# A decoder layer in one kernel: the down-projection's fast passes reordered, and its last two column chunks made a fourth fast pass

## The chip, the cores and the metric

The kernel runs on one core of one Trainium2 chip. It is one program that computes a whole decoder layer for 256 tokens. The metric is the device time of one execution in microseconds (us). An engine name in the profile stands for: PE TensorE's matmuls, PEld its weight loads, DVE VectorE, ACT ScalarE, POOL GpSimd, SP SyncE, which issues most of the transfers.

## The reference

The layer has a token mixer (two kinds of attention side by side) and a channel mixer. Only the end of the channel mixer is touched by the change:

```python
h = rmsnorm(x, pre_ffn_g[l])
u = causal_dwconv(h @ w_up[l], conv_w[l], conv_b[l])          # 2048 -> 2 x 5632
gate, val = jnp.split(u, 2, axis=-1)
y = (jax.nn.gelu(gate, approximate=True) * val) @ w_down[l]   # 5632 -> 2048
x = x + rmsnorm(y, post_ffn_g[l])
```

There are 256 tokens, in two tiles of 128. Everything is float32. The last line needs the mean square over all 2048 columns of y for each token, so no token's output can be written before its whole row of y is known.

## The kernel before

**Products in three matmuls.** Every float32 matrix product is made of three reduced-precision matmuls: each operand is split into a high part (a cast on ScalarE) and a low part (source minus high part, on VectorE), and high x high, high x low and low x high are added up in PSUM. `product` (L964) does this for a 128x128 block on the left and up to 512 columns on the right; `mm3` (L305) does the same in the plain passes. `split` (L311) makes a pair of parts, and so does `w_split` (L102) behind `w_unit` (L120). The split weights lie in two rings `whi` and `wlo` of five buffers each; a buffer is free when TensorE has read it for the last time.

**Two halves.** The 5632 inner columns are done in two halves of 22 tiles of 128. In each half, 11 turns of the up-projection (two weight groups each, gate and value) make the 22 tiles `G[0..21]`, by matmul, convolution, GELU and product; the convolution works in a tile called `room`. Then the half's part of the down-projection is done, in passes over column ranges of `w_down`. Partial results gather in `y_sb`.

**A fast pass.** `fast_pass` (L969) covers 1024 columns. It goes over 11 pairs of inner tiles. A plain pair needs 2x2x2 = 8 products (two inner tiles, two token tiles, two column chunks), 24 matmuls of 512 columns. For the four pairs in `FAST` it uses a Strassen-like scheme with seven products, 21 matmuls: the four sums of token tiles are made once per half by `token_sums` and kept in `sums`, and four differences of the weight blocks (L1004 to L1010, into the tile `tb`) are made on VectorE for each pair in each pass, then split like weights. Of the seven products, four gather in the PSUM banks `early`, whose sums are added to `y_sb` by `add_early` when the last fast pair is done; the others gather in the banks `late`, together with the plain pairs, and are added block by block by `add_late` in the pass's last pair.

**Which passes there are.** Half 0 has two fast passes (columns 0 to 1023, 1024 to 2047). Half 1 has one fast pass (0 to 1023), then a plain pass over chunk 2 (columns 1024 to 1535), then the plain pass over chunk 3 (1536 to 2047), which is written out separately at the end. In the first pass of each half the pairs come in the order 1, 0, 3, 2, 5, 4, 7, 6, 8, 9, 10, in the others from 0 to 10.

**The last chunk.** It does token tile 0 for all 11 pairs first, and the other tile for the first five pairs (`LAST = 11 - HOLD`, `HOLD = 6`), in two halves of 256 columns with a bank each. The split weights of the last six pairs are kept (four in the rings, two in rooms that are free by then, `rest`). While these last products of token tile 1 run on TensorE, tokens 0 to 127 are finished.

**Finishing.** In half 1, `down` (L1074) takes a finished bank: VectorE adds it to `y_sb`, ScalarE squares it and sums up the row (`ysq`), and GpSimd multiplies it by the gain `gbf` (L1079). When a token tile has all its columns, `before_last` and `rstd_y` make the inverse root (VectorE, then a power on GpSimd), and `finish` (L1162) multiplies, adds the residual `x_back` and writes out.

**Transfers.** Weights come in pieces of 512 KB on SP's queue, in order. In the fast passes eight buffers take turns: five of the ring `raw`, two of `extra`, one third of `tb` (which lies in the convolution's `room`). The residual comes back from `x_dram` into `x_back`, two transfers of 1 MB, during the last passes; it lies in the room that `sums` had.

**What sets the order.** TensorE's order is the program's own throughout. On the other engines a planner orders the instructions by its own estimate of when each can start, up to the last stage (from the second `manual_schedule`); from there all engines keep the program's order.

Of the kernel before, what the change touches and what calls it, by code (L numbers as in the profile page):

```python
# [17 lines left out]
P = 128  # L18
# [7 lines left out]
FHALF = 22  # L26
HOLD = 6
FAST = (0, 2, 4, 6)
# [3 lines left out]
def hybrid_layer(ctx: ExitStack, tc: tile.TileContext, x, pre_mix_g, w_in, b_forget, sinks,  # L32
# [16 lines left out]
    def bank(tag="acc"):  # L49
        return ps.tile([P, 512], F32, tag=tag, bufs=4, name="bank_" + tag)  # L50
# [796 lines left out]
    with tc.tile_pool(name="ffn", bufs=1) as fp:  # L847
# [115 lines left out]

        def product(b, lh, ll, rhs, cols, first, last):  # L964
            hi, lo = rhs
            for i, (a, r) in enumerate(((lh, hi), (lh, lo), (ll, hi))):
                pe.matmul(b, a, r[:, cols], start=(first and i == 0), stop=(last and i == 2))  # L967

        def fast_pass(G, sums, order, k00, c0, load, tb, early, late, add_early, add_late):  # L969

# [6 lines left out]
            def parts(src, n):  # L977
                hi, lo = w_parts(n)
# [5 lines left out]
            started = set()  # L984

            def first(bk):
                new = id(bk) not in started
                started.add(id(bk))
                return new

            for u in order:
                k = 2 * u
                ra, rb = (load(w_rows(w_down, k00 + k + a, 1, c0, UNIT)) for a in range(2))
                if u in FAST:
# [38 lines left out]

        ysq = [small.tile([P, 5], F32, tag=f"ysq{t}", bufs=1, name=f"ysq{t}") for t in range(2)]
        gbf = None
        for half in range(2):
# [44 lines left out]

            LAST = FHALF // 2 - HOLD
            extra = fp.tile([P, 2, UNIT], F32, tag="gbc", name="extra")
# [11 lines left out]

            for n in range(0, 2 if half else 4, 2):
                early, late = ([bank(tag) for _ in range(4)] for tag in ("acc", "att"))
                order = list(range(FHALF // 2))
                if n == 0:
                    order[:8] = [1, 0, 3, 2, 5, 4, 7, 6]  # L1100

                def y_of(t, c):
                    return y_sb[:, t, (n + c) * 512:(n + c + 1) * 512]
# [20 lines left out]

                def add_late(t, c, b):
# [5 lines left out]
                fast_pass(G, sums, order, half * FHALF, n * 512, load, tb, early, late, add_early,  # L1131
                          add_late)
            for n in range(2, 2 + half):
                b2 = [bank(), bank()]
                for u in range(FHALF // 2):
                    hi, lo = w_unit(w_rows(w_down, half * FHALF + u * 2, 2, n * 512, 512), 2, 512)
                    for a in range(2):
                        k = u * 2 + a
                        for t in range(2):
                            mm3(b2[t], G[k], t, hi[:, a, :], lo[:, a, :], slice(0, 512), k == 0,  # L1140
                                k == FHALF - 1)
                for t in range(2):
                    down(t, n, b2[t])

# [17 lines left out]
        def finish(t, cs, r, q, y=None):  # L1162
# [3 lines left out]

        rest = [fp.tile([P, 2, UNIT], F32R, tag="gbc", name="rest"),
                fp.tile([P, ROOM], F32R, tag="room", name="rest")[:, 544:544 + 2 * UNIT]
                .rearrange("p (a c) -> p a c", a=2)]
        x_back = main.tile([P, 2, D], F32, tag="x", name="x_back")  # L1170
        b0, b1 = bank(), [bank(), bank()]
        halves = [slice(0, 256), slice(256, 512)]
        held = []
        for u in range(FHALF // 2):
            if u in (1, 2):
                sp.dma_start(x_back[:, u - 1, :], x_dram[(u - 1) * P:u * P, :])
            hi, lo = w_unit(w_rows(w_down, FHALF + u * 2, 2, 1536, 512), 2, 512,
                            keep=(None, [rest[u - LAST][:, i, :] for i in range(2)])
                            if LAST <= u < FHALF // 2 - 4 else None)
            for a in range(2):  # L1180
                k = u * 2 + a
                args = (k, hi[:, a, :], lo[:, a, :])
                held.append(args)
                mm3(b0, G[k], 0, *args[1:], slice(0, 512), k == 0, k == FHALF - 1)
                for h in range(2 if u < LAST else 0):
                    mm3(b1[h][:, halves[h]], G[k], 1, *args[1:], halves[h], k == 0, False)
# [49 lines left out]
```

## Time and profile before

| | us |
|---|---|
| median of 3 runs | 1079.45 |
| lowest and highest | 1078.14, 1080.15 |
| the profiled execution's own time | 1077.63 |
| its span, first to last instruction | 1075.6 |
| half 0's two fast passes | 584.05 to 644.50, 644.50 to 701.78 |
| half 1's fast pass | 944.05 to 1006.06 |
| its plain passes over chunks 2 and 3 | 1006.06 to 1067.08 |
| after TensorE's last matmul | 1067.08 to 1075.60 |

Times in the lines of the profile are microseconds from the start of the span; in a line of the timeline the first number is the start, the second the length of the stretch, and `x3` the number of instructions in it. What stands in brackets is how long the engine was idle before it and which instruction ended that. Matmuls are pipelined, so a single one is listed with 0.39 us although one starts every 0.23.

### The profile page before, as it was taken

How to read it: one execution, taken by the hardware profiler on the slowest of the kernel's cores; microseconds unless marked ns; L12 is line 12 of the kernel's file. 1: busy time of each engine (PE TensorE's matmuls, PEld its weight loads, DVE VectorE, ACT ScalarE, POOL GpSimd, SP SyncE). 2: the span in 40 equal slices, each digit the busy share in tenths (PEclk: the TensorE clock that was granted, in tenths of full speed). 3: DMA queues.
4: the chain of work that ended last, by engine and by line, in shares of the span. 5: the costliest groups of instructions: out<-in, count | busy, mean ns of one | idle time of the engine just before them, and what ended most of it. 6: DMA issues, size and time to landing. Idle time of an engine off the chain costs nothing.

```text
span 1075.6 us, 16358 instructions
## 1 busy us (share of the span) xinstructions
PE 1056.9 (98%) x5950; PEld 919.1 (85%) x5950; DVE 822.4 (76%) x1336; ACT 630.7 (59%) x1087; POOL 224.9 (21%) x256
## 2 busy tenths in 40 slices
PE   9999999999999999999999999999999999989996
PEld 7899988887889888888888788888888888878886
DVE  5988878887567887788777989668777787779763
ACT  7766766666556765656554645456565555555450
POOL 4343243332022121212121000012121212100211
PEclk9999999999999999999999999999999999999998
DMA  8646556554873876656664666666566656555752
GB/s 291 206 122 177 176 157 209 162 161 157 293 236 105 283 226 195 191 184 191 192 191 138 219 206 215 214 180 194 178 213 189 187 184 198 189 192 179 280 168 79
DMA packets 157100, 207.09 MB, mean 193 GB/s; under 512 B 6844, under 2 KB 131036, under 8 KB 155996
## 3 DMA queue, kind: packets, MB, share of 16 engines
q1 hardware_dynamic: 156016, 203.37, 60.2%
q10 hardware_dynamic: 1004, 2.68, 0.6%
q8 instruction: 47, 0.77, 0.3%
q14 instruction: 33, 0.27, 0.1%
HBM read 201.68 MB, written 4.21 MB: 191 GB/s over the span
## 4 chain that ended last, share of the span: by engine, by line
PE 89%; DVE 4%; ACT 2%; DMA 2%; POOL 2%; issue 1%; SPq 0%; POOLq 0%; DVEq 0%; ACTq 0%
PE bank_acc L309 18%; PE bank_acc L284 16%; PE bank_att L284 14%; PE bank_att L967 12%; PE bank_acc L290 8%; PE bank_att L290 7%; PE bank_acc L253 4%; PE bank_acc L967 3%; PE bank_acc L258 2%; DVE wlo L115 2%; PE bank_att L475 1%; POOL scr L442 1%; PE bank_att L510 1%; PE bank_acc L932 1%; DMA x_in<-in_x_dram 1%
## 5 line engine op out<-in xcount | busy, mean ns | idle before, releaser
L115 DVE TENSOR_TENSOR wlo<-raw,whi 128x1024 fp32r<-128x1024 f32 (+3 forms) x291 | 358.6, 1242 | 133.2 <-ACT whi L112 128.5
L112 ACT CAST whi<-raw 128x1024 fp32r<-128x1024 f32 (+3 forms) x290 | 294.4, 1031 | 149.6 <-issue 88.8
L899 POOL TENSOR_TENSOR room<-room,rowf 128x256 f32<-128x256 f32 x88 | 99.4, 1150 | 393.1 <-DVE room L898 391.5
L284 PE MATMUL bank_acc<-hT,whi 128*128 128x512 f32 x736 | 173.3, 390 | 0.0
L284 PEld LDWEIGHTS bank_acc<-hT,whi 128*128 128x128 f32 x736 | 136.4, 188 | 27.4
L284 PE MATMUL bank_att<-hT,whi 128*128 128x512 f32 x640 | 150.6, 390 | 0.0
L284 PEld LDWEIGHTS bank_att<-hT,whi 128*128 128x128 f32 x640 | 118.7, 188 | 23.9
L967 PE MATMUL bank_att<-whi,G 128*128 128x512 f32 x384 | 122.5, 389 | 0.0
L290 PEld LDWEIGHTS bank_acc<-hT,wlo 128*128 128x128 f32 x736 | 89.3, 188 | 2.0
L290 PE MATMUL bank_acc<-hT,wlo 128*128 128x256 f32 x736 | 89.8, 279 | 0.0
L253 PE MATMUL bank_acc<-hT,whi 128*128 128x512 f32 x352 | 89.2, 396 | 0.0
L901 ACT ACTIVATE room<-room,cw 128x256 f32<-128x256 f32 x88 | 53.0, 602 | 60.1 <-POOL room L899 59.9
L967 PEld LDWEIGHTS bank_att<-whi,G 128*128 128x128 f32 x384 | 72.2, 188 | 15.1
L309 PE MATMUL bank_acc<-whi,oT 128*128 128x512 f32 (+1 forms) x272 | 82.5, 380 | 0.0
L290 PEld LDWEIGHTS bank_att<-hT,wlo 128*128 128x128 f32 x640 | 77.6, 188 | 1.7
L290 PE MATMUL bank_att<-hT,wlo 128*128 128x256 f32 x640 | 77.9, 279 | 0.0
L903 DVE SCALAR_TENSOR_TENSOR room<-room,cw 128x256 f32<-128x256 f32 x88 | 61.9, 703 | 19.4 <-ACT room L901 19.4
L967 PE MATMUL bank_att<-wlo,G 128*128 128x512 f32 x192 | 74.7, 389 | 0.0
L253 PEld LDWEIGHTS bank_acc<-hT,whi 128*128 128x128 f32 x352 | 62.9, 188 | 11.3
L309 PEld LDWEIGHTS bank_acc<-whi,oT 128*128 128x128 f32 x272 | 50.2, 188 | 9.3
L313 DVE TENSOR_TENSOR wlo<-raw,whi 128x1024 fp32r<-128x1024 f32 (+1 forms) x44 | 49.5, 1149 | 9.4 <-ACT whi L312 9.3
L312 ACT CAST whi<-raw 128x1024 fp32r<-128x1024 f32 (+1 forms) x44 | 42.4, 991 | 21.3 <-PE bank_att L967 15.9
(252 smaller groups left out, 1613.8 us busy)
## 6 DMA issues: line engine op xcount, KB each, us to landing
raw<-in_w_up_dram SPq DMA_DIRECT2D x176, 512.0 KB, 4.2
raw<-in_w_down_dram SPq DMA_DIRECT2D x66, 512.0 KB, 4.6
raw<-in_w_in_dram SPq DMA_DIRECT2D x51, 512.0 KB, 4.2
raw<-in_w_out_dram SPq DMA_DIRECT2D x32, 512.0 KB, 4.5
extra<-in_w_down_dram SPq DMA_DIRECT2D x15, 512.0 KB, 4.9
raw<-in_w_in_dram SPq DMA_DIRECT2D x16, 384.0 KB, 3.3
tb<-in_w_down_dram SPq DMA_DIRECT2D x7, 512.0 KB, 3.7
cb<-c_dram SPq DMA_DIRECT2D x8, 256.0 KB, 3.7
```

The costliest lines, as they stand in the source:

```text
L112: i1 = act.copy(hi[:, cs], raw[:, cs])
L115: i2 = dve.tensor_tensor(lo[:, cs], raw[:, cs], hi[:, cs].bitcast(F32), op=ALU.subtract)
L253: pe.matmul(b, parts[u][0][:, a, m * P:(m + 1) * P], hT[:, kt, :], start=(kt == 0), stop=(kt == KT - 1))
L284: pe.matmul(b, parts[u][0][:, a, m * P:(m + 1) * P], hT[:, kt, :], start=(kt == 0), stop=(kt == KT - 1))
L290: pe.matmul(b[:, 256:512], parts[u][1][:, a, m * P:(m + 1) * P], hT[:, kt, 0:256], start=False, stop=False)
L309: pe.matmul(b, a, r[:, cols], start=(first and i == 0), stop=(last and i == 2))
L312: act.copy(hi, src)
L313: dve.tensor_tensor(lo, src, hi.bitcast(F32), op=ALU.subtract)
L899: pool.tensor_tensor(u[:, 2:258], u[:, 2:258], rowf, op=ALU.mult)
L901: act.activation(y, u[:, 2:258], AF.Identity, bias=cw[:, 3, ch:ch + 1], scale=cw[:, 2, ch:ch + 1])
L903: dve.scalar_tensor_tensor(y, u[:, 1:257], cw[:, 1, ch:ch + 1], y, op0=ALU.mult, op1=ALU.add)
L967: pe.matmul(b, a, r[:, cols], start=(first and i == 0), stop=(last and i == 2))
```

## The change

- **The order in each half's first pass** becomes 1, 3, 0, 5, 2, 7, 4, 8, 6, 9, 10: two plain pairs come before the first fast one, and two instead of three are left after the last.
- **A second fast pass in half 1** over columns 1024 to 2047 takes the place of the two plain passes. It uses the same `sums`, so these stay until its last fast pair is done.
- **Its last three pairs are held** (`HOLD = 3`): they are split like the others, but their products come after all the rest, block by block (`block`): token tile 0 chunk 2, tile 0 chunk 3, tile 1 chunk 2, tile 1 chunk 3, each 18 matmuls of 512 columns, the last one as two times 18 of 256 in a bank of its own. What had gathered in the fourth bank before is added to `y_sb` on VectorE first. Four of the six held weight rows lie in the rings, the last pair's two in `rest`, which now takes the room of `sums`.
- **`add_late` is gone**: in the other passes the last pair goes through `block` too, in the same order of matmuls as before, and the banks are added after it.
- **`x_back`** lies behind the gain in the tile that took `hT`'s place, and its two transfers are issued ahead of the fourth pass's loads.
- **The finish** has two more `down` steps, those of chunk 2, in the program's own order between the blocks.

```diff
-HOLD = 6
+HOLD = 3
...
-        def product(b, lh, ll, rhs, cols, first, last):
+        def product(b, lh, ll, rhs, cols, first, last, to=None):
             hi, lo = rhs
             for i, (a, r) in enumerate(((lh, hi), (lh, lo), (ll, hi))):
-                pe.matmul(b, a, r[:, cols], start=(first and i == 0), stop=(last and i == 2))
+                pe.matmul(b[:, to] if to else b, a, r[:, cols], start=(first and i == 0),
+                          stop=(last and i == 2))
...
-                b = [parts(ra, UNIT), parts(rb, UNIT)]
-                blocks = ((p2, 0, left), (p3, 0, right), (p4, 1, left), (p22, 1, right))
-                end = u == order[-1]
-                order2 = ([(a, x) for x in blocks for a in range(2)] if end else
-                          [(a, x) for a in range(2) for x in blocks])
-                for a, (bk, t, cols) in order2:
-                    product(bk, *of(k + a, t), b[a], cols, first(bk), end and a == 1)
-                    if end and a == 1:
-                        add_late(t, 1 if cols is right else 0, bk)
+                b = [parts(r, UNIT, keep[a] if keep and u == order[-1] else None)
+                     for a, r in enumerate((ra, rb))]
+                if u in order[-hold:]:
+                    held += [(k + a, b[a]) for a in range(2)]
+                    continue
+                for a in range(2):
+                    for bk, t, cols in blocks:
+                        product(bk, *of(k + a, t), b[a], cols, first(bk),
+                                hold > 1 and bk is p22 and u == order[-hold - 1] and a == 1)
+
+            def block(i, bk=None, cols=None):
+                b, t, c = blocks[i]
+                for n, (k, w) in enumerate(held):
+                    product(bk or b, *of(k, t), w, cols or c, bk is not None and n == 0,
+                            n == len(held) - 1, cols and slice(cols.start - 512, cols.stop - 512))
+
+            return block
...
-                gbf = main.tile([P, 4 * D], F32, tag="hT", name="gbc_ffn")[:, 0:D]
+                late_room = main.tile([P, 4 * D], F32, tag="hT", name="late_room")
+                gbf = late_room[:, 0:D]
+                x_back = late_room[:, D:3 * D].rearrange("p (t c) -> p t c", t=2)
...
-            for n in range(0, 2 if half else 4, 2):
+            for n in (0, 2):
                 early, late = ([bank(tag) for _ in range(4)] for tag in ("acc", "att"))
                 order = list(range(FHALF // 2))
                 if n == 0:
-                    order[:8] = [1, 0, 3, 2, 5, 4, 7, 6]
+                    order[:9] = [1, 3, 0, 5, 2, 7, 4, 8, 6]
+                elif half:
+                    for t in range(2):
+                        sp.dma_start(x_back[:, t, :], x_dram[t * P:(t + 1) * P, :])
...
+                final = half and n
+                rest = None
+                if final:
+                    rest = main.tile([P, 2, 2, UNIT], F32R, tag="x", name="rest")
+                block = fast_pass(G, sums, order, half * FHALF, n * 512, load, tb, early, late,
+                                  add_early, HOLD if final else 1,
+                                  rest and [[rest[:, a, i, :] for i in range(2)]
+                                            for a in range(2)])
+                if final:
+                    dve.tensor_tensor(y_of(1, 1), late[3], y_of(1, 1), op=ALU.add)
+                    break
+                for i in range(4):
+                    block(i)
+                    t, c = divmod(i, 2)
                     if half:
-                        down(t, n + c, b)
+                        down(t, n + c, late[i])
                     else:
-                        dve.tensor_tensor(y_of(t, c), b, y_of(t, c), op=ALU.add)
...
-            for n in range(2, 2 + half):
-                b2 = [bank(), bank()]
-                for u in range(FHALF // 2):
-                    hi, lo = w_unit(w_rows(w_down, half * FHALF + u * 2, 2, n * 512, 512), 2, 512)
...
+        block(0)
+        down(0, 2, late[0])
         v = before_last(0, 3)
-        down(0, 3, b0)
+        block(1)
+        down(0, 3, late[1])
         r = rstd_y(0, 3, v)
         for n in range(4):
             finish(0, slice(n * 512, (n + 1) * 512), r, sp)
+        block(2)
+        down(1, 2, late[2])
         last = fp.tile([P, 256], F32, tag="last", name="last")
         for h in range(2):
             if h:
                 v = before_last(1, 4)
-            for k, hi, lo in held[LAST * 2:]:
-                mm3(b1[h][:, halves[h]], G[k], 1, hi, lo, halves[h], False, k == FHALF - 1)
-            down(1, 3, b1[h], h, last if h else None)
+            b = bank()
+            block(3, b, slice(512 + h * 256, 768 + h * 256))
+            down(1, 3, b, h, last if h else None)
```

More of the change, by code (lines that the diff above doesn't have):

```diff
@@ L962, in token_sums, with fast_pass @@
             split(into[:, 0:512], into[:, 512:UNIT], s.rearrange("p k c -> p (k c)"))
-        def product(b, lh, ll, rhs, cols, first, last):
+        def product(b, lh, ll, rhs, cols, first, last, to=None):
             hi, lo = rhs
             for i, (a, r) in enumerate(((lh, hi), (lh, lo), (ll, hi))):
-                pe.matmul(b, a, r[:, cols], start=(first and i == 0), stop=(last and i == 2))
-        def fast_pass(G, sums, order, k00, c0, load, tb, early, late, add_early, add_late):
+                pe.matmul(b[:, to] if to else b, a, r[:, cols], start=(first and i == 0),
+                          stop=(last and i == 2))
+        def fast_pass(G, sums, order, k00, c0, load, tb, early, late, add_early, hold=1,
+                      keep=None):
             left, right = slice(0, 512), slice(512, UNIT)
@@ L975, in of, with parts @@
                 return G[k][:, t * P:(t + 1) * P], G[k][:, 256 + t * P:256 + (t + 1) * P]
-            def parts(src, n):
-                hi, lo = w_parts(n)
+            def parts(src, n, into=None):
+                hi, lo = into or w_parts(n)
                 split(hi, lo, src)
@@ L983, in fast_pass @@
             p2, p3, p4, p22 = late
-            started = set()
+            blocks = ((p2, 0, left), (p3, 0, right), (p4, 1, left), (p22, 1, right))
+            started, held = set(), []
             def first(bk):
@@ L1080, in down @@
                                    gbf[:, n * 512:(n + 1) * 512][:, cs], op=ALU.mult)
-            LAST = FHALF // 2 - HOLD
             extra = fp.tile([P, 2, UNIT], F32, tag="gbc", name="extra")
@@ L1123, in add_early @@
                     dve.tensor_tensor(y_of(1, 1), s, y_of(1, 1), op=ALU.add)
-                def add_late(t, c, b):
+                final = half and n
[12 more added lines that the diff above has]
+                    t, c = divmod(i, 2)
                     if half:
-                        down(t, n + c, b)
+                        down(t, n + c, late[i])
                     else:
-                        dve.tensor_tensor(y_of(t, c), b, y_of(t, c), op=ALU.add)
-                fast_pass(G, sums, order, half * FHALF, n * 512, load, tb, early, late, add_early,
-                          add_late)
-            for n in range(2, 2 + half):
-                b2 = [bank(), bank()]
-                for u in range(FHALF // 2):
-                    hi, lo = w_unit(w_rows(w_down, half * FHALF + u * 2, 2, n * 512, 512), 2, 512)
[L1137 to L1143, printed above, removed]
+                        dve.tensor_tensor(y_of(t, c), late[i], y_of(t, c), op=ALU.add)
         def before_last(t, n):
@@ L1165, in finish @@
             q.dma_start(of[t * P:(t + 1) * P, cs], y_sb[:, t, cs])
[L1167 to L1186, printed above, removed]
         ctx.enter_context(tc.manual_schedule(
```

## The prediction

> **What bounds the kernel now.** I read the page's busy shares first, then what TensorE waited for, then a table by stage, then the timelines around the stages that the change touches.
>
> ```profile
> PE 1056.9 (98%) x5950; PEld 919.1 (85%) x5950; DVE 822.4 (76%) x1336; ACT 630.7 (59%) x1087; POOL 224.9 (21%) x256
> ```
>
> TensorE sets the end. Time can be won only from matmuls, from its few waits, or after its last matmul. Its waits:
>
> ```profile
> PE bank_acc L967 <- ACT whi L312: 3.7, 2, 1.9
> PE bank_acc L967 <- DVE wlo L313: 1.8, 2, 0.9
> ```
>
> L967 is the fast products; two waits each means one pair in each half's first pass. By stage (length, then busy time and count of PE, PEld, DVE, ACT, POOL, then PE clock, DMA share, GB/s):
>
> ```profile
> 584.05:644.50 60.45, 57.70 (x253) 47.23 (x252) 55.74 (x71) 32.06 (x38) 1.34 (x2) 1.00 0.57 192
> 644.50:701.78 57.28, 57.28 (x254) 47.47 (x253) 43.73 (x47) 30.23 (x32) 0.20 (x4) 1.00 0.63 211
> 944.05:1006.06 62.01, 59.26 (x253) 48.36 (x252) 53.92 (x67) 34.13 (x42) 2.80 (x4) 0.97 0.63 219
> 1006.06:1036.00 29.94, 29.94 (x133) 24.77 (x132) 18.78 (x15) 15.42 (x18) 5.34 (x3) 1.00 0.66 212
> 1036.00:1067.08 31.08, 31.05 (x199) 28.11 (x197) 14.49 (x19) 7.88 (x14) 6.10 (x5) 1.00 0.27 89
> 1067.08:1075.60 8.52, 0.00 (x0) 0.00 (x0) 3.54 (x7) 0.51 (x2) 1.27 (x2) 0.66 0.35 123
> ```
>
> Rows 1 and 2 are the two passes of half 0, row 3 the first pass of half 1, rows 4 and 5 the plain passes over column chunks 2 and 3, row 6 the tail. A fast pass has 4x7x3 + 7x8x3 = 252 matmuls of 512 columns. Row 2, with PE busy throughout, prices one at 57.28 / 252 = 0.2273 us, so a plain pair (24) lasts 5.45 and a fast pair (21) 4.77. Row 5 has 66 of 512 columns and 132 of 256: (31.08 - 66 x 0.2273) / 132 = 0.122 us for a 256.
>
> **Part 1: two plain pairs in front.** Against row 2, the same work costs 3.17 us more in row 1 and 4.73 more in row 3: 7.90 in all. In half 1 this is TensorE, and the clock after it:
>
> ```profile
> 949.96 0.39 PE L967 MATMUL bank_acc<-whi,G 128*128 128x512 f32 x1
> 952.21 0.50 PE L967 MATMUL bank_acc<-whi,sums 128*128 128x512 f32 x1 [1.87 <-ACT whi L312]
> 953.60 0.71 PE L967 MATMUL bank_acc<-wlo,sums 128*128 128x512 f32 x1 [0.88 <-DVE wlo L313]
> ```
>
> ```profile
> 954.00:957.20 3.20, 3.20 (x9) 2.43 (x9) 3.20 (x4) 2.85 (x4) 0.00 (x0) 0.51 0.27 90
> ...
> 590.00:596.00 6.00, 3.25 (x14) 2.17 (x13) 5.96 (x8) 4.61 (x5) 0.00 (x0) 1.00 0.52 179
> ```
>
> The waits of half 1 are followed by a granted clock of 0.51, those of half 0 by 1.00; this is the 1.56 us between 4.73 and 3.17. [...] I count it as going, because it follows the wait at once.
>
> Why TensorE waited: one plain pair lasts until 949.5, and VectorE is not yet there:
>
> ```profile
> 944.44 0.76 DVE L898 TENSOR_TENSOR room<-bank_acc,room 128x256 f32<-128x256 f32 x2 [4.24 <-ACT room L897]
> ...
> 948.77 0.98 DVE L313 TENSOR_TENSOR G<-room,G 128x256 fp32r<-128x256 f32 x2
> 949.79 0.69 DVE L1004 TENSOR_TENSOR tb<-raw 128x512 f32<-128x512 f32 x1
> 950.40 0.69 DVE L1005 TENSOR_TENSOR tb<-raw 128x512 f32<-128x512 f32 x1
> ...
> 952.33 2.42 DVE L313 TENSOR_TENSOR wlo<-tb,whi 128x1024 fp32r<-128x1024 f32 x2
> ```
>
> The differences (0.61 apart) need the room of the convolution, which ends at 949.75; the two split sums are there at 953.5 and 954.7. With pair 3 in between, TensorE comes to pair 0 at 944.05 + 2 x 5.45 = 954.95, wants the first sum's low part after four matmuls (955.9) and the second after nine (957.0). Slack 2.3 us at both. What is added before that: pair 3's two splits, 2 x 1.21. The ring of five split buffers lets the first be made where pair 0's quarter was made before, and the second when the last projection frees a buffer, inside the 4.24 us VectorE idles. Were all of it, and the quarter's 0.6, to come behind the convolution, the chain would be up to 3.0 later, that is 0.7 over the slack. So I take -7.90, bounds -7.90 and -6.5. Half 0 shows the same picture.
>
> Loads: the order of the first eight changes, and the eighth waits for the convolution's room on SP's queue, with all later loads behind it:
>
> ```profile
> 949.83 0.33 SPq L1093 DMA_DIRECT2D tb<-in_w_down_dram  x1
> 951.11 6.26 SPq L69 DMA_DIRECT2D raw<-in_w_down_dram  x3
> ```
>
> ```profile
> raw<-in_w_down_dram SPq DMA_DIRECT2D x66, 512.0 KB, 4.6
> ```
>
> Pair 2, formerly loads 7 and 8, becomes 9 and 10: issued 2.1 apart, the last lands at 951.11 + 2.1 + 4.6 = 957.8. TensorE needs its first sum at 944.05 + 5.45 + 5.45 + 4.77 + 5.45 + 0.9 = 966.1, and from the landing to that sum it takes 0.6 + 1.0 + 1.2. Slack over 5 us, cost nothing.
>
> **Part 2: the fourth pass.** Removed: 264 matmuls' worth in rows 4 and 5, 29.94 + 31.08 = 61.02 us. Added: 234 of 512 and, in the last block, 36 of 256: 234 x 0.2273 + 36 x 0.122 = 57.58. Difference -3.44 us: twelve products' worth of 512 columns is 2.73, the rest is the smaller number of 256s.
>
> VectorE's load grows. A fast pair needs four differences and about 3.5 splits, 2.4 + 4.2 = 6.6 us, a plain pair 2.4, together 9.0 against TensorE's 10.2. It keeps up, but at the boundary of half 1's passes it gets crowded. Pair 6 used to have three plain pairs behind it and a plain pass after them; now it has two and a fast pair. Pair 6 ended at 1006.06 - 3 x 5.45 = 989.7, and the first addition of the seven products' sums was
>
> ```profile
> 987.49 0.69 DVE L1116 TENSOR_TENSOR y_sb<-s,y_sb 128x512 f32<-128x512 f32 x1
> ```
>
> 2.2 before that end. From there VectorE has, at 0.61 an addition or difference and 1.2 a split: 8 additions 4.9, pair 10's splits 2.4, the next pair's differences 2.4, its quarter 0.6, its two sums 2.4, three late additions 1.8: 14.5 us, done 12.3 after pair 6. TensorE needs the second sum 2 x 5.45 + 9 x 0.2273 = 12.95 after it. Slack 0.65. Against it stand GpSimd's multiplications (L1079) of the first pass, which fell on idle VectorE time before:
>
> ```profile
> 1004.93 0.69 DVE L1077 TENSOR_TENSOR y_sb<-bank_att,y_sb 128x512 f32<-128x512 f32 x1 [0.57 <-PE bank_att L967]
> 1006.29 0.69 DVE L1077 TENSOR_TENSOR y_sb<-bank_att,y_sb 128x512 f32<-128x512 f32 x1 [0.67 <-PE bank_att L967]
> 1006.90 7.14 DVE L115 TENSOR_TENSOR wlo<-raw,whi 128x1024 fp32r<-128x1024 f32 x4
> ```
>
> ```profile
> 1004.60 2.55 POOL L1079 TENSOR_TENSOR y_sb<-y_sb,gbc_ffn 128x512 f32<-128x512 f32 x2 [58.31 <-ACT junk L1078]
> 1007.37 4.25 POOL L1079 TENSOR_TENSOR y_sb<-y_sb,gbc_ffn 128x512 f32<-128x512 f32 x2 [0.22 <-ACT junk L1078]
> ```
>
> Four splits took 7.14 instead of 4.8: 2.3 us lost beside 4.25 of GpSimd; the addition that reads PSUM stayed at 0.69. One to two splits before the second sum, and the ones for the rest of pair 0 and for pair 1 right after, lose 0.6 each. I take +1.3 us of waiting (about three splits' loss less the slack), bounds 0 (it fits) and 4. Half 0 has half the additions there and no multiplications: nothing.
>
> At the end of the pass, pairs 8 to 10 are held, pair 10 in the room of the token sums, so its casts on ScalarE wait for pair 6's last product, with only pair 10's second cast behind them. VectorE has from 2.2 before that: 8 additions, 5 splits and one late addition, 11.5 us, done 9.3 after pair 6; TensorE needs the last low part 5.45 + 16 x 0.2273 = 9.1 after it. About nothing; bounds 0 and 1.5. The two reads of the residual, 1.05 MB each, now stand ahead of the pass's loads on SP's queue: at 211 GB/s up to 9.9 us of traffic. The loads run eight buffers, some 20 us, ahead, so I cost them at nothing; without that cover, 9.9.
>
> **Part 3: the tail.** Now chunk 2's sums fall into it too.
>
> ```profile
> 1058.45 0.69 DVE L1077 TENSOR_TENSOR y_sb<-bank_acc,y_sb 128x512 f32<-128x512 f32 x1 [8.69 <-PE bank_acc L309]
> 1059.99 0.16 DVE L1157 SCALAR_TENSOR_TENSOR rv<-ysq,rv 128x1 f32<-128x1 f32 x1 [0.85 <-ACT junk L1078]
> 1061.87 2.74 DVE L1163 SCALAR_TENSOR_TENSOR y_sb<-y_sb,ry,x_back 128x512 f32<-128x512 f32 x4 [1.72 <-POOL ry L1159]
> ```
>
> ```profile
> 1060.04 1.29 POOL L1079 TENSOR_TENSOR y_sb<-y_sb,gbc_ffn 128x512 f32<-128x512 f32 x1 [18.51 <-ACT junk L1078]
> 1061.29 0.55 POOL L1159 TENSOR_TENSOR ry<-rv,mhalf 128x1 f32<-128x1 f32 x1
> 1065.63 0.74 POOL L1079 TENSOR_TENSOR y_sb<-y_sb,gbc_ffn 128x256 f32<-128x256 f32 x1 [3.79 <-ACT junk L1078]
> 1067.59 0.73 POOL L1079 TENSOR_TENSOR last<-y_sb,gbc_ffn 128x256 f32<-128x256 f32 x1 [1.22 <-DVE y_sb L1077]
> 1068.41 0.55 POOL L1159 TENSOR_TENSOR ry<-rv,mhalf 128x1 f32<-128x1 f32 x1
> ```
>
> Let E be TensorE's end (1067.08 here). Tokens 0 to 127 were ready at E - 8.6, their four last steps ended at E - 2.5. After the change they are ready at E - 18 x 0.2273 - 36 x 0.122 = E - 8.5, so the steps end at E - 2.4. Behind them on VectorE now come chunk 2's addition (0.7) and then the first 256's. ScalarE's square of the former ends near E - 0.8, GpSimd's 1.29 runs to E + 0.5, its two 0.74s to E + 2.0, and the power behind them ends at E + 2.5 instead of 1068.96 - 1067.08 = E + 1.9. +0.65 us, bounds +0.2 and +1.2.
>
> **Sum**, against the profiled execution's 1077.63 (span 1075.6 and 2.0 around it): -7.90 - 3.44 + 1.3 + 0.65 = -9.4, so 1068.2. The median of the runs, 1079.45, stands 1.8 above that execution; I forecast it to stay so: 1070.0.
>
> **Rivals.** (a) VectorE loses GpSimd's whole time. Rows: 2.3 of 4.25 lost, not all. If the four multiplications of 1.29 each cost VectorE their length, 5.2 less the slack of 0.65 is 4.5 of waiting, 3.2 more than forecast: 1073.2. [...] (b) The opening wait only moves to the second fast pair, because loads 9 and 10 come late. It begins at 5 us of lateness; for it speak the 6.26 us for three loads, against it that VectorE has slack everywhere after 953.6. As long as the old gaps, it gives back most of 7.90: 1077. (c) Slower than before: the residual's reads sit on SP's queue until GpSimd has finished with the gain in the same tile (1007.37 + 4.25, 5.6 us after the pass), and all loads of the fourth pass behind them. Then 9.9 of traffic, 4.6 of landing and 3.4 of preparing: 23 us of idle TensorE, about 1092; from 11 us on it decides the sign. Against it: at 1004.93 VectorE writes one slice of y_sb while GpSimd works on another, so waits go by slices.
>
> **Chances.** Forecast 0.64, own range 1068.3 to 1071.8; (a) 0.21; (b) 0.09; (c) 0.06. The range 1067.0 to 1074.5 takes in the first two and the bounds of the terms. A measurement of this kernel tells 0.2%, 2.2 us, from no change: faster 0.89, within it 0.05, slower 0.06.
>
> **What would show it.** The changed profile should have no wait of TensorE on pair 0 of the first passes, stages of 57.3 us with clock 1.00 there, TensorE ending its fourth pass 57.6 us plus any wait after the third, a wait of one to two us at that pass's first fast pair on a VectorE split, and a tail near 9.2 us. A wait of over 4 us there, a wait at pair 2 of an opening, or SP's loads stopped behind the residual would make it wrong.

## The result, and the profile after

| | before | after |
|---|---|---|
| median, us | 1078.80 (6 runs) | 1071.22 (6 runs) |
| lowest and highest | 1077.16, 1080.15 | 1070.06, 1072.17 |
| the profiled execution | 1077.63, span 1075.6 | 1070.95, span 1069.2 |

The ratio is 0.9931, with a 95% interval of 0.9918 to 0.9943: the changed kernel is 7.6 us faster. The prediction was 1070.0, with a range of 1067.0 to 1074.5.

TensorE's waits in the down-projection, from the profile after (total, number, longest):

```profile
PE bank_att L967 <- DVE wlo L313: 2.4, 2, 1.8
PE bank_att L967 <- DVE rest L313: 1.1, 2, 0.8
```

The waits of the openings, on `bank_acc`, are gone. Four others have come, all on `bank_att` and all on low parts from VectorE. The table by stage shows where they are (columns as in the prediction: stretch and length, then busy time and count of PE, PEld, DVE, ACT, POOL, then PE clock, DMA share, GB/s):

```profile
583.97:641.08 57.11, 57.11 (x253) 47.30 (x252) 53.29 (x69) 31.11 (x37) 1.79 (x2) 1.00 0.61 198
641.08:698.30 57.22, 57.22 (x253) 47.23 (x252) 45.07 (x49) 30.03 (x32) 0.20 (x4) 1.00 0.63 210
...
940.74:997.86 57.12, 57.12 (x253) 47.31 (x252) 53.68 (x70) 31.71 (x39) 2.56 (x3) 1.00 0.74 254
997.86:1060.24 62.38, 58.89 (x271) 47.81 (x269) 52.69 (x64) 30.18 (x42) 9.81 (x8) 1.00 0.38 127
1060.24:1069.20 8.96, 0.00 (x0) 0.00 (x0) 3.51 (x8) 0.51 (x2) 2.39 (x4) 0.68 0.34 117
```

Rows 1 and 3 are the two openings. Both run through at a clock of 1.00, and are 3.34 and 4.89 us shorter than before. Row 4 is the new fourth pass: 62.38 us, where the two plain passes took 61.02. It has fewer matmuls than they had and still takes 1.36 us longer. TensorE in that pass, from the timeline (start, length, and in brackets the idle time before it):

```profile
1003.44 0.50 PE L967 MATMUL bank_att<-wlo,G 128*128 128x512 f32 x1 [1.79 <-DVE wlo L313]
...
1005.67 0.50 PE L967 MATMUL bank_att<-wlo,G 128*128 128x512 f32 x1 [0.57 <-DVE wlo L313]
...
1045.24 0.97 PE L967 MATMUL bank_att<-rest,G 128*128 128x512 f32 x3 [0.31 <-DVE rest L313]
...
1046.97 0.73 PE L967 MATMUL bank_att<-rest,G 128*128 128x512 f32 x2 [0.77 <-DVE rest L313]
```

Two waits stand at the start of the pass, the first for pair 0's plain weight row (the last of the four splits that this pair needs), the second for pair 1's first row. Two stand in the first of the held blocks, for pair 10's two low parts. Each costs more than its listed length: the idle time is counted from the end of the matmul before, 0.39 us after its start, where the next would have started after 0.23, and from the matmul behind the wait to the next one it is 0.34 (1003.44 to 1003.78). From the pass's first matmul to pair 2's it takes 13.14 us (997.86 to 1011.00), where 45 matmuls at 0.2273 us are 10.23: 2.9 us lost for 2.36 us of waiting. VectorE around the first two, and GpSimd beside it, in the same profile:

```profile
996.77 0.68 DVE L1090 TENSOR_TENSOR y_sb<-bank_att,y_sb 128x512 f32<-128x512 f32 x1
997.38 2.09 DVE L313 TENSOR_TENSOR wlo<-tb,whi 128x1024 fp32r<-128x1024 f32 x1
999.39 0.68 DVE L1090 TENSOR_TENSOR y_sb<-bank_att,y_sb 128x512 f32<-128x512 f32 x1
999.99 1.18 DVE L1007 TENSOR_TENSOR tb<-raw 128x512 f32<-128x512 f32 x1
1001.09 0.68 DVE L1090 TENSOR_TENSOR y_sb<-bank_att,y_sb 128x512 f32<-128x512 f32 x1
1001.69 1.70 DVE L313 TENSOR_TENSOR wlo<-tb,whi 128x1024 fp32r<-128x1024 f32 x1
1003.31 2.31 DVE L313 TENSOR_TENSOR wlo<-raw,whi 128x1024 fp32r<-128x1024 f32 x1
```

```profile
997.09 3.53 POOL L1092 TENSOR_TENSOR y_sb<-y_sb,late_room 128x512 f32<-128x512 f32 x2 [53.40 <-ACT junk L1091]
1000.96 1.34 POOL L1092 TENSOR_TENSOR y_sb<-y_sb,late_room 128x512 f32<-128x512 f32 x1 [0.34 <-ACT junk L1091]
1002.66 1.88 POOL L1092 TENSOR_TENSOR y_sb<-y_sb,late_room 128x512 f32<-128x512 f32 x1 [0.35 <-ACT junk L1091]
```

VectorE is never idle here. A split whose two inputs lie in SBUF takes 1.22 us by itself (1015.21 in `e3_no_gain`, below) and 2.09, 1.70 and 2.31 beside GpSimd's multiplications by the gain, a difference 1.18 instead of 0.68 (1016.95 there). The additions that take one input from PSUM (L1090) stay at 0.68. The splits end at 1003.39 and 1005.62, and TensorE goes on at 1003.44 and 1005.67.

### The profile page after: what moved, and what is told of

It reads as the page before. It is cut to its first block, busy times and chain, and to the rows that moved or that the text cites. A ratio compares the mean times of both kernels' runs of the same rounds, so it can differ in the third digit from the quotient of the medians.

```text
span 1069.2 us, 16290 instructions
## 1 busy us (share of the span) xinstructions
PE 1052.4 (98%) x5890; PEld 912.9 (85%) x5890; DVE 843.4 (79%) x1369; ACT 637.2 (60%) x1096; POOL 224.8 (21%) x256
## 4 chain that ended last, share of the span: by engine, by line
PE 90%; DVE 4%; DMA 2%; issue 2%; POOL 1%; ACT 1%; SPq 0%; DVEq 0%; POOLq 0%; ACTq 0%
PE bank_acc L284 16%; PE bank_att L967 14%; PE bank_att L284 14%; PE bank_acc L309 12%; PE bank_acc L290 8%; PE bank_att L290 7%; PE bank_acc L253 6%; PE bank_acc L967 4%; PE bank_acc L258 3%; PE bank_att L475 1%; DVE wlo L313 1%; PE bank_att L510 1%; DVE wlo L115 1%; PE bank_acc L932 1%; DMA x_in<-in_x_dram 1%
## 5 line engine op out<-in xcount | busy, mean ns | idle before, releaser
L115 DVE TENSOR_TENSOR wlo<-raw,whi 128x1024 fp32r<-128x1024 f32 (+3 forms) x271 | 330.1, 1228 | 117.1 <-ACT whi L112 112.4
L112 ACT CAST whi<-raw 128x1024 fp32r<-128x1024 f32 (+3 forms) x270 | 273.3, 1029 | 124.4 <-issue 88.9
L967 PE MATMUL bank_att<-whi,G 128*128 128x512 f32 x488 | 156.2, 389 | 0.0
L967 PEld LDWEIGHTS bank_att<-whi,G 128*128 128x128 f32 x488 | 91.6, 188 | 18.9
L967 PE MATMUL bank_att<-wlo,G 128*128 128x512 f32 x244 | 95.2, 390 | 2.4 <-DVE wlo L313 2.4
L313 DVE TENSOR_TENSOR wlo<-raw,whi 128x1024 fp32r<-128x1024 f32 (+1 forms) x56 | 62.4, 1138 | 13.4 <-ACT whi L312 13.4
L312 ACT CAST whi<-tb 128x1024 fp32r<-128x1024 f32 x42 | 44.0, 1050 | 45.0 <-PE bank_att L967 19.2
L312 ACT CAST whi<-raw 128x1024 fp32r<-128x1024 f32 (+1 forms) x56 | 52.4, 958 | 28.8 <-PE bank_att L967 22.2
```

The lines of the kernel that those rows point to most:

```text
L112: i1 = act.copy(hi[:, cs], raw[:, cs])
L115: i2 = dve.tensor_tensor(lo[:, cs], raw[:, cs], hi[:, cs].bitcast(F32), op=ALU.subtract)
L312: act.copy(hi, src)
L313: dve.tensor_tensor(lo, src, hi.bitcast(F32), op=ALU.subtract)
L967: pe.matmul(b[:, to] if to else b, a, r[:, cols], start=(first and i == 0), stop=(last and i == 2))
```

## The experiments

Ratios are against the kernel before on the same chip. A fourth pass is measured from the end of half 1's first pass to VectorE's addition of the last 256 columns; the tail is the rest of the span.

**The order alone** (run `e1_order_alone`): the kernel before, with one line.

```diff
-                    order[:8] = [1, 0, 3, 2, 5, 4, 7, 6]
+                    order[:9] = [1, 3, 0, 5, 2, 7, 4, 8, 6]
```

> The kernel before with the new pair order in the two first passes, and nothing else. Theory: all of the gain of the change comes from here. Both opening waits go and the clock dip with them, so each first pass starts its next stage 57.1 us after its start: 3.3 us less in half 0, 4.9 in half 1, the rest as before: -8.2 us, ratio 0.9924. Rival (the fourth pass carries a part of the gain, and the order alone makes the plain pass behind it wait): -5 us or less, ratio 0.995 or more.

Measured: 1068.91 us (4 runs), ratio 0.9908 (0.9895 to 0.9922). No wait of TensorE on L967 is left. The part that was to bring most is there on its own, and the kernel with only this part stands no higher than the whole change: beside it, the fourth pass brought nothing. The median fell by 10.1 us where 8.2 were expected; the section on the prediction comes back to this.

**The fourth pass alone** (run `e2_pass_alone`): the changed kernel with the old order of the first passes.

```diff
-                    order[:9] = [1, 3, 0, 5, 2, 7, 4, 8, 6]
+                    order[:8] = [1, 0, 3, 2, 5, 4, 7, 6]
```

> The changed kernel with the old pair order in the first passes (1, 0, 3, 2, ...), so three plain pairs stand behind the last fast one. [...] The fourth pass has 3.4 us less of matmul, waits at its start for 0 to 1.5 us since there is one more plain pair of cover, and at its end for 1.75; the tail is 0.4 longer: together -1.3 to 0 us against before, ratio 0.9988 to 1.000. Rival (the two parts need each other): slower than before by 1 us or more.

Measured: 1078.81 us (11 runs), ratio 0.9996 (0.9987 to 1.0005), no change. Rows by stage of this run: half 0's opening pass, then 4 us behind the gap in each half, then the fourth pass:

```profile
584.71:646.67 61.96, 59.20 (x254) 48.34 (x252) 55.91 (x71) 32.21 (x38) 1.34 (x2) 0.97 0.56 187
```

```profile
594.00:598.00 4.00, 3.75 (x10) 2.99 (x11) 4.00 (x5) 3.50 (x5) 0.00 (x0) 0.57 0.36 119
956.00:960.00 4.00, 4.00 (x12) 3.12 (x12) 4.00 (x4) 3.01 (x4) 0.00 (x0) 0.59 0.93 323
```

```profile
1008.28:1068.65 60.37, 58.69 (x271) 47.87 (x269) 49.85 (x62) 29.98 (x40) 8.04 (x7) 1.00 0.39 131
```

Two things are to be seen. First, with the old order the fourth pass takes 60.37, not 62.38: three plain pairs stand behind pair 6 in the pass before, VectorE comes to the boundary with more in hand (the split of pair 0's second sum ends 1.9 us before the pass begins, at 1006.36, and in the changed kernel 1.6 us after it, at 999.47), and of the first two waits one of 0.58 us is left. So the parts work against each other: the order that helps the openings takes a plain pair from the end of the same pass, and that costs 2.0 us at the next pass's start. Second, the clock behind the opening's gap falls in both halves here (0.57 and 0.59); in the profiled execution of before it fell in half 1 alone.

**GpSimd's multiplications later** (run `e4_gain_later`): the four multiplications by the gain are issued only when pair 3 of the fourth pass is split, VectorE's order being that of the changed kernel.

```diff
             def down(t, n, b, h=None, into=None):
...
+                if n < 2:
+                    gains.append((ys, gbf[:, n * 512:(n + 1) * 512]))
+                    return
...
+                def give_gains(w):
+                    z = small.tile([P, 1], F32, tag="st", name="z_gain")
+                    i = pool.tensor_scalar(z, w[:, 0:1].bitcast(F32), 0.0, None, op0=ALU.mult)
+                    with tc.issue_after(i.ins):
+                        for y, g in gains:
+                            pool.tensor_tensor(y, y, g, op=ALU.mult)
```

> The changed kernel, with the four multiplications by the gain that GpSimd does for columns 0 to 1023 queued behind a one-column instruction that reads pair 3's split weight in the fourth pass, so that they run in the middle of that pass instead of at its start. The order of VectorE's instructions is the same as in the changed kernel. Theory (GpSimd in VectorE's way): the two waits at the start of the fourth pass, 1.79 and 0.57 us, go, VectorE's splits there are 1.22 long again instead of 1.7 to 2.3, and the middle of the pass absorbs the same loss: -2.5 to -2.9 us against the changed kernel, ratio to before 0.9905. Rival (VectorE has simply too much queued there: eight additions, four late ones, and a difference of pair 2 ahead of the split that is wanted): the waits stay, ratio 0.993.

Measured: 1071.88 us (5 runs), ratio 0.9932 (0.9919 to 0.9946): the same as the whole change. The waits at the start of the pass are gone, and a new one has come up at its third fast pair. TensorE, VectorE and GpSimd there, from this run's timeline:

```profile
1023.53 0.50 PE L967 MATMUL bank_acc<-whi,sums 128*128 128x512 f32 x1 [2.17 <-ACT whi L312]
1024.79 0.50 PE L967 MATMUL bank_acc<-wlo,sums 128*128 128x512 f32 x1 [0.76 <-DVE wlo L313]
```

```profile
1013.18 2.91 DVE L313 TENSOR_TENSOR wlo<-extra,whi 128x1024 fp32r<-128x1024 f32 x2
1016.01 2.31 DVE L313 TENSOR_TENSOR wlo<-tb,whi 128x1024 fp32r<-128x1024 f32 x1
1018.25 1.78 DVE L1011 TENSOR_TENSOR tb<-tb 128x512 f32<-128x512 f32 x1
1019.95 1.78 DVE L1008 TENSOR_TENSOR tb<-raw 128x512 f32<-128x512 f32 x1
```

```profile
1013.32 7.85 POOL L1155 TENSOR_TENSOR y_sb<-y_sb,late_room 128x512 f32<-128x512 f32 x4
```

The loss has moved with the multiplications, and the expected gain of 2.5 to 2.9 us did not come. VectorE has no room for them beside the fast pairs at either of the two places tried.

**Without the multiplications** (run `e3_no_gain`): as the changed kernel, but columns 0 to 1023 are not multiplied by the gain.

> The change, with GpSimd's four multiplications by the gain for columns 0 to 1023 of the last two token halves left out (so the output lacks the gain in these columns). The theory: their being beside VectorE's splits is what makes TensorE wait 1.79 + 0.57 us at the start of half 1's fourth pass and lose some 2.9 us there with the restarts. Then the two waits go, no wait comes up later in the pass (unlike the run that only moved them), the waits for the kept splits (0.31, 0.77) stay, the fourth pass takes 59.0 to 59.9 us in place of 62.4, and the time is 1068 to 1069 us. The rival, that the pass's first pair has too much VectorE work behind the additions of the third pass whatever GpSimd does: the splits there still end late, at least 1.2 us of the wait stays, 1070 to 1071 us.

Measured: 1068.94 us (4 runs), ratio 0.9909 (0.9894 to 0.9923). At the start of the pass one wait of 0.32 us is left, none comes up at a later fast pair, the two on `rest` stay (0.31 and 0.76), and the pass takes 59.86:

```profile
998.42:1058.28 59.86, 58.42 (x271) 47.94 (x269) 50.17 (x65) 30.41 (x42) 3.84 (x4) 1.00 0.39 132
```

That is 2.5 us below the changed kernel's 62.38. From the pass's first matmul to pair 2's it takes 10.82 us (998.42 to 1009.24) instead of 13.14, so of the 2.9 us lost there 0.6 are left: the multiplications beside VectorE are the cause of most of the loss at the start. The same four VectorE stretches as in the run before, now without GpSimd:

```profile
1013.48 1.82 DVE L313 TENSOR_TENSOR wlo<-extra,whi 128x1024 fp32r<-128x1024 f32 x2
1015.21 1.22 DVE L313 TENSOR_TENSOR wlo<-tb,whi 128x1024 fp32r<-128x1024 f32 x1
1016.35 0.69 DVE L1011 TENSOR_TENSOR tb<-tb 128x512 f32<-128x512 f32 x1
1016.95 0.68 DVE L1008 TENSOR_TENSOR tb<-raw 128x512 f32<-128x512 f32 x1
```

They take 4.15 us here (1013.48 to 1017.63), and 8.55 beside GpSimd (1013.18 to 1021.73).

**The additions later** (run `e5_adds_later`): as the changed kernel, but in the pass with held pairs the eight additions of the `early` banks are emitted behind the splits of the last pairs.

```diff
-                    if end:
+                    if end and hold == 1:
                         add_early()
...
+            if hold > 1:
+                add_early()
```

> The change, with the eight additions of the fourth pass's early banks issued behind the splits of its last three pairs in place of ahead of them. The theory: the waits for the kept splits (0.31 and 0.77 us, some 1.7 with the restarts) go and the waits at the pass's start stay, so the pass takes 60.6 us and the time is 1069.5 us. The rival, that a late addition then delays the end: the additions run on into the last block, the tail grows by as much, 1071 us, no change from the whole change.

Measured: 1070.07 us (4 runs), ratio 0.9917 (0.9902 to 0.9932). The two waits on `rest` are gone, those at the start stay (1.01 and 0.56 here), and the tail does not grow:

```profile
999.61:1059.57 59.96, 58.33 (x271) 47.96 (x269) 52.16 (x64) 29.41 (x40) 9.39 (x7) 1.00 0.40 132
1059.57:1068.50 8.93, 0.00 (x0) 0.00 (x0) 3.51 (x8) 0.51 (x2) 2.39 (x4) 0.77 0.34 117
```

The pass is 2.42 us shorter than the changed kernel's, of which 0.79 are the shorter waits at the start in this execution; about 1.6 is what the waits on `rest` cost, with what is lost around them. By time alone, the two intervals overlap.

**Both moved** (run `e6_both`): the multiplications as in `e4_gain_later` and the additions as in `e5_adds_later`.

> As the one before, and the additions of the four products in the fourth pass come after the splits of its last pairs in the program, so that the planner prefers the splits. Theory: the waits for the last pair's low parts in the first held block (0.31 and 0.77 us, 1.75 with what is lost around them) go too: ratio to before 0.989, about 1067. Rival (those splits are late because of the buffers and casts, not the additions, or the additions now delay the steps of the tail): no gain over the one before, 0.9905, or a longer tail.

Measured: 1070.08 us (4 runs), ratio 0.9920 (0.9906 to 0.9933). The expected ratio, 0.989, was missed: the waits on `rest` are gone, but those at the third fast pair stay with 2.04 and 0.77. The clock of the 4 us behind them, in this run and then in `e4_gain_later`, where the waits were 2.17 and 0.76:

```profile
1025.00:1029.00 4.00, 4.00 (x13) 3.11 (x13) 4.00 (x5) 2.75 (x4) 0.00 (x0) 0.65 0.46 143
```

```profile
1025.00:1029.00 4.00, 4.00 (x18) 3.10 (x18) 4.00 (x5) 2.80 (x4) 0.00 (x0) 1.00 0.43 138
```

**Plain pairs in front of the fourth pass too** (run `e7_plain_first_both`): `e5_adds_later`, and in this pass two plain pairs come first, with the two groups of banks exchanged, since the banks that plain pairs write would otherwise still wait for the pass before.

```diff
-                early, late = ([bank(tag) for _ in range(4)] for tag in ("acc", "att"))
+                tags = ("att", "acc") if half and n else ("acc", "att")
+                early, late = ([bank(tag) for _ in range(4)] for tag in tags)
                 order = list(range(FHALF // 2))
+                if half and n:
+                    order[:6] = [1, 3, 0, 2, 5, 4]
...
-            b = bank()
+            b = bank("att")
             block(3, b, slice(512 + h * 256, 768 + h * 256))
```

> The run above, and the fourth pass too begins with two plain pairs (order 1, 3, 0, 2, 5, 4, 6 and on), with the two groups of banks exchanged in this pass, so that the plain pairs write banks that have long been free. A plain pair asks VectorE for two differences of 1.22 us each (2.3 with GpSimd beside them) in 6.8 us of TensorE, so VectorE can lose the 2.9 us to GpSimd and still be ahead. The theory: no wait longer than 0.3 us in the whole pass, 57.6 to 58 us, 1066 to 1067 us: below the order alone (1068.9). The rival, that VectorE is short over the whole pass and not only at its start: the wait comes up at the fast pairs 0 and 2, one behind the other, with 2 us or more, and the time stays at 1068.5 to 1069.5 us.

Measured: 1067.57 us (4 runs), ratio 0.9897 (0.9880 to 0.9914). One wait of 0.20 us is left in the pass, in the first held block, and the pass takes 58.20, just above the expected 57.6 to 58; the waits that the rival named did not come. (A plain pair asks VectorE for two splits, where the expectation says differences, and TensorE takes 5.45 us for it, not 6.8.) The exchange of the banks was not run by itself. Since this stood only 1.3 us below the order alone, on another chip, both ran once more on one chip.

**The last two again, side by side** (runs `e8_order_again` and `e9_plain_first_again`).

> The kernel before with the new order of the first passes alone, a second time, to stand beside the next kernel on one chip. By the stages: two plain passes of 60.97 us and a tail of 8.57, 69.54 us from the end of half 1's first pass. 1068.9 us.

> The kernel with two plain pairs at the front of the fourth pass too and its additions later, a second time. By the stages: the fourth pass 58.18 us and a tail of 9.01, 67.19 us from the end of half 1's first pass, 2.35 less than the order alone. If the seven products are worth this, it stands 2 to 2.5 us below the order alone on the same chip, 1066.6 us; if the gap between the two first runs (1067.57 and 1068.91, on different chips) was the chips, they agree within 0.7 us.

Measured: 1070.11 us (1069.24 to 1070.48, 5 runs) for the order alone, ratio 0.9921 (0.9908 to 0.9933), and 1066.86 us (1066.42 to 1067.44, 4 runs) for the other, ratio 0.9891 (0.9876 to 0.9907). Their runs do not overlap: the medians lie 3.25 us apart. What follows half 1's first pass, first in the order alone (two plain passes, tail), then in the other (fourth pass, tail):

```profile
998.84:1059.82 60.98, 60.95 (x331) 52.89 (x329) 34.12 (x35) 23.16 (x31) 11.88 (x8) 1.00 0.49 166
1059.82:1068.30 8.48, 0.00 (x0) 0.00 (x0) 3.54 (x7) 0.51 (x2) 1.27 (x2) 0.75 0.35 124
```

```profile
998.36:1056.56 58.20, 57.94 (x271) 47.95 (x269) 53.96 (x69) 29.18 (x40) 9.60 (x7) 1.00 0.37 127
1056.56:1065.50 8.94, 0.00 (x0) 0.00 (x0) 3.51 (x8) 0.51 (x2) 2.38 (x4) 0.72 0.34 117
```

With the waits gone the seven products bring 2.78 us, less 0.46 in the tail: 2.32 of the 3.25. Another 0.48 lies ahead of this stage (998.84 against 998.36); the rest is not placed. VectorE in `e9_plain_first_again` at the start of the pass:

```profile
996.83 2.10 DVE L313 TENSOR_TENSOR wlo<-raw,whi 128x1024 fp32r<-128x1024 f32 x1
998.85 1.28 DVE L1093 TENSOR_TENSOR y_sb<-bank_att,y_sb 128x512 f32<-128x512 f32 x2
1000.05 2.91 DVE L313 TENSOR_TENSOR wlo<-raw,whi 128x1024 fp32r<-128x1024 f32 x2
1002.88 1.77 DVE L1007 TENSOR_TENSOR tb<-raw 128x512 f32<-128x512 f32 x1
```

VectorE loses to GpSimd as before (2.10 for 1.22, 1.77 for 0.68, beside multiplications at 996.55 to 1004.10), but TensorE now needs only two splits for every 5.45 us, and it does not wait at the start of the pass. This version is faster than both kernels. What the loss would be with the multiplications moved into the tail wasn't tried.

## Why the prediction was right, and where it was not

The forecast, 1070.0, came 1.2 us below the median of 1071.22, with errors of 3.5 us (the fourth pass) and 1.5 us (the step to the median) that partly cancel. That it came so close is in part luck; that the openings bring the gain is not.

| term | predicted | in the profiles |
|---|---|---|
| openings | -7.90 | -8.23 (3.34 + 4.89) |
| fourth pass: matmuls, start, held pairs | -3.44 + 1.3 + 0 = -2.14 | +1.36 |
| tail | +0.65 | +0.44 |
| time around the span | 0 | -0.28 (2.03 to 1.75) |
| sum on the profiled execution | -9.4 | -6.68 |
| from there to the median | +1.8 | +0.27 |

**Part 1, the openings: right.** No wait at pair 0, clock 1.00, 57.11 and 57.12 us where 57.3 was said. Taking the dip of the clock as a part of the gap held too: with the gap gone, it shows in neither half. What I had not followed through is the offset to the median. The old order loses 3.3 us in a half without a dip (60.45 against 57.11) and 4.9 with one (61.96 in `e2_pass_alone`). The profiled execution of before had one dip, that of `e2_pass_alone` two. An execution of before with two would lie some 1.5 us above the profiled one (an estimate, 61.96 - 60.45), and the median of the three runs then known lay 1.8 above it (that of all six 1.2). So the step "the median stands 1.8 above that execution; I forecast it to stay so" failed, and to the good: the changed kernel's median is only 0.27 above its profiled execution. Only profiled executions show the clock by stage, but the mean clock of every execution beside the experiments is on record, and it bears this out. Of 31 executions of before, the six with a mean clock of 0.996, that of the profiled one, took 1076.90 to 1077.79 us; the other 25, with 0.994 or 0.995, took 1078.31 to 1080.07. `e2_pass_alone`, seen with two dips, had 0.994. So most executions of before had two dips, as far as a mean can tell, and the new order saves such an execution about 9.7 us by the same estimate (8.23 + 1.5), which is most of what `e1_order_alone` gained beyond its expectation (10.1 against 8.2; on another chip `e8_order_again` gained 8.7).

**Part 2, the start of the fourth pass: the mechanism right, the size wrong.** A wait on VectorE's splits at the first fast pair was predicted and came. The step that failed is "Slack 0.65 ... I take +1.3 us": the slack was counted at pair 0's second sum, and there it held, as the sum's split ended at 999.47 and TensorE did not stop. But the next split, of pair 0's plain row, came behind two late additions and pair 2's difference, and it had no slack: without any GpSimd work (`e3_no_gain`) TensorE still waited 0.32 us for it. Then VectorE lost 0.87 + 0.50 + 0.48 us on the way to it, and 1.09 on the next: 2.9 in place of the three times 0.6 that I had priced. The price came from a misread row. It was 2.3 us shared out over four splits, but what stood beside them were two multiplications, and now there were four. The prediction also set the 2.3 against 4.25 us of GpSimd, though in the 4.25 the two multiplications were slowed themselves; the two ahead of them took 2.55 with almost only additions from PSUM beside them. Against 2.55, VectorE had lost nearly the whole of GpSimd's time even there. The waits of 1.79 and 0.57, with what is lost around them, cost 2.9 us, inside the bounds of 0 and 4.

**Part 2, the held pairs: at the edge of its bound or just past it.** "About nothing; bounds 0 and 1.5": 0.31 and 0.77 us of waiting, and pair 10's six matmuls of the first block take 3.01 us (1044.54 to 1047.55) instead of 1.36, about 1.6 lost. My count put VectorE 0.2 us late, with 8 additions, 5 splits and one late addition in 11.5 us. In the profile after, 8 additions and 7 splits lie between the first addition and the last low part (1034.09 to 1046.92), 12.8 us: the count had two splits too few (and one addition too many). The waits went as soon as the additions stood behind the splits (`e5_adds_later`): the additions had no hurry at all, while the splits did.

**Part 2, the matmuls: right.** `e9_plain_first_again`, with one wait of 0.2 us left, ran the pass in 58.20 where 57.58 was worked out. (The "twelve products" of the prediction are twelve matmuls, those of four products; the 2.73 us are right.)

**The tail: right** (0.44, bounds 0.2 to 1.2), by the step that was named: the power waits behind GpSimd's multiplications, which run to 1062.1 in the profile after, 1.9 after the last addition began:

```profile
1059.49 1.96 POOL L1092 TENSOR_TENSOR y_sb<-y_sb,late_room 128x512 f32<-128x512 f32 x2 [4.27 <-ACT junk L1091]
1061.40 0.72 POOL L1092 TENSOR_TENSOR last<-y_sb,late_room 128x256 f32<-128x256 f32 x1
1062.09 0.54 POOL L1171 TENSOR_TENSOR ry<-rv,mhalf 128x1 f32<-128x1 f32 x1
```

**The rivals.** (a), that VectorE loses GpSimd's whole time, came nearer than I had it. In the changed kernel VectorE lost 2.9 us for four multiplications that take 1.29 each by themselves, 5.2 in all. In `e4_gain_later`, where only splits and differences run beside them, it lost 8.55 - 4.15 = 4.4. The share depends on what VectorE runs: beside additions from PSUM neither loses much (0.69 for an addition and 2.55 for two multiplications in the profile of before). So (a) is nearly right where VectorE reads SBUF twice (4.4 of the 5.2). That at the boundary the additions in between kept it from coming true in full fits this, but no run tested it. (b), the wait moved to the second fast pair, did not come: no wait in either opening pass. (c), SP's queue stopped by the residual, did not come either; the planner issued both reads some 50 us before the pass, as SP's timeline shows:

```profile
941.89 0.42 SPq L1115 DMA_DIRECT2D late_room<-x_dram  x1
...
948.71 1.40 SPq L1115 DMA_DIRECT2D late_room<-x_dram  x1
```

So the sign rested on the openings alone, as `e1_order_alone` and `e2_pass_alone` show. By the stages the changed kernel is 1.9 us behind the order alone (62.38 + 8.96 against 60.98 + 8.48); by time the intervals of the two overlap.

## What to carry to other kernels

When a step is reordered to fill the start of a stage, count what it takes from the end of that stage: the pair moved to the front was the cover for the next stage's start. When slack is counted on a busy engine, follow it to each later consumer until the engine idles, not only to the first. Work with fewer matmuls but more preparation wants its lightest pieces where the preparing engine is shortest of time, and a helper engine's work beside it can be charged to that engine: here, where GpSimd and VectorE both read SBUF twice, VectorE lost 4.4 us to GpSimd's 5.2 (`e4_gain_later`).

## What the runs showed of the hardware

- Splits and differences of VectorE and multiplications of GpSimd, each reading SBUF twice, took nearly as long side by side as one after the other: work of 4.15 us on VectorE and 4 x 1.29 = 5.2 on GpSimd, 9.3 in all, took 8.55 us, 92% of it (1013.18 to 1021.73 in `e4_gain_later`). In the profile of before, four splits (4.8 us) beside two multiplications (2.55) took 7.14. VectorE's additions with one input from PSUM stayed at 0.68 us beside such multiplications (999.39 and 1001.09 in the profile after).
- The same gap of TensorE was followed by a lower clock at some times and not at others. Waits of 2.75 us in two steps were followed by 1.00 in half 0 of before, by 0.51 in half 1, and by 0.57 and 0.59 in `e2_pass_alone`; 2.93 by 1.00 in `e4_gain_later`, 2.81 by 0.65 in `e6_both`. The fall cost some 1.5 us on top of the wait (61.96 in `e2_pass_alone` against 60.45 before, for the same pass), so that the old order lost 4.9 us with the fall and 3.3 without (57.11 after). What decides it is open: of these gaps, the longest single idle stretch behind which the clock fell is 2.04 us (`e6_both`), and behind one of 2.17 us it did not (`e4_gain_later`).
